# A sliding-window copy kernel: opening load in four DMAs, halved copies placed otherwise, last stores in parts

## Chip, cores, metric

One core of one Trainium2 chip. The metric is the device time of one execution in microseconds (us), smaller is better.

## The reference

```python
# x: (32, 4096, 256) float32, window_size 64, stride 32  ->  out: (32, 127, 64, 256)
for i in range(n_windows):                 # n_windows = (4096 - 64) // 32 + 1 = 127
    start = i * stride
    result[:, i] = x[:, start:start + window_size].copy()
```

There is no arithmetic. A *block* is 32 rows of 256 floats, 32 KB. Window i of a batch is blocks i and i+1, so nearly every block is written twice. 134 MB are read, 266 MB are written.

## The kernel before

The kernel has two ways to move data. Both start and end in HBM, the chip's main memory. Eleven of the 32 batches are *staged*: loaded into SBUF, the core's on-chip memory, once (4 MB, one block a partition) and stored twice, once as first halves and once as second halves of the windows. The other 21 are *direct*: copied from HBM to HBM, 16 windows in one DMA. A staged batch costs the DMA engines three transfers of 4 MB for 8 MB of output, a direct one costs them only the 8 MB of output, but reads every block twice from HBM. (The page of before has 138.41 MB on ScalarE's queue, 33 transfers of 4.19 MB, and 220.95 MB read from HBM: 46.1 by the staged loads, 174.8 by direct copies and edges.) Three queues issue: ScalarE (ACT) the staged loads and stores, SyncE (SP) the direct copies, GpSimd (POOL) at the end the *edges*, windows that a staged store of a neighbouring batch has overwritten with wrong blocks and that must be copied after it.

```python
DIRECT, IN, OUT = 32768, 16384, 16384      # largest piece (descriptor) in bytes

class Staging:
    def load(self, q, g):
        n, i = divmod(g, len(self.tiles))          # 6 tiles
        if n:
            q.wait_ge(self.stored[i], 32 * n)
        self.c.load(q, self.tiles[i], ...).then_inc(self.loaded[i], 16)      # 128 x 32 KB

    def store(self, q, g):
        n, i = divmod(g, len(self.tiles))
        q.wait_ge(self.loaded[i], 16 * (n + 1))
        for half in (0, 1):
            self.c.store(q, self.tiles[i], ..., half, ...).then_inc(self.stored[i], 16)
    # ... run(): six loads, their stores, five loads, their stores
...
    per, loads, stores = 6, 6 * 17, 34
    todo = 7 * len(direct)                          # 147 copies of 16 windows
    turns = share = 0
    with tc.tile_critical():
        st.run(ring_s)                              # ScalarE's queue
        for b in direct:
            w = ...
            for j in range(7):
                todo -= 1
                sem = near if todo == 2 else done
                share += 90 if turns % (loads + per * stores) < loads else 12
                if share >= 120:                    # halved: two DMAs of 16 x 32 KB
                    share -= 120
                    turns += 4
                    count(c.windows(ring_d, b, w, 16, 0), done)
                    count(c.windows(ring_d, b, w, 16, 1), sem)
                else:                               # whole: one DMA of 16 x (2 x 32 KB)
                    turns += 3
                    count(c.windows(ring_d, b, w, 16), sem)
                w += 16
                ...
        ring_r.wait_ge(near, 16)
        ...                                         # edges on GpSimd's queue, each after its stores
        count(c.windows(ring_r, last, 112, 4), rest)
        count(c.columns(ring_r, last, 116, 9), rest)
        st.wait_stored(ring_d, len(staged) - 1)
        count(c.columns(ring_d, last, 125, 2), done)          # 128 KB, after the last store
        for sem in (done, near, rest):
            ring_d.wait_ge(sem, total[sem])
```

`turns` is bookkeeping: a turn is one packet, and a packet that writes a completion counts too. It rests on what the traces show: while both queues are full, they start the same number of packets, 2910 on SyncE's and 2911 on ScalarE's from 150 to 400 us, beside stores, and 1177 and 1173 from 20 to 110 us, beside loads (before, completion writes included). Per engine a whole copy is two data packets and a completion (3 turns for 64 KB), a halved one is 4 turns for 64 KB, a staged load or store is 16 packets of 16 KB and a completion (17 turns for 256 KB). By this counting, halving slows the direct queue against the staged one. The shares fit: beside stores it gives the direct queue 57.8% of the bytes, and 57.6% were measured (before, 150 to 400 us); beside loads, where three of four copies are halved, 53%. With 11 staged batches fixed, halving is the lever by which the kernel sets the mix.

Of the kernel before, what the change touches and what calls it, by code (L numbers as in the profile page):

```python
# [11 lines left out]
class Copier:  # L12


    def __init__(self, x, out, B, L, D, W, S, n_win):
        assert W == 2 * S and L % S == 0
        self.x, self.out = x, out
        self.B = B
        self.blk = S * D
        self.nb = L // S  # L20
        self.nw = n_win
# [24 lines left out]
            in_=self.xap(b * self.nb + w0, [[part, 16], [self.blk, n], row]),  # L46
        )

    def load(self, q, t, b, shift):

        return q.dma_start(
            out=t[:, :],
            in_=self.xap(b * self.nb - shift, [[self.blk, self.nb], [1, self.blk]]),
            max_dma_last_dim=IN,
        )

    def store(self, q, t, b, half, shift):


        w = b * self.nw - half - shift  # L60
        return q.dma_start(
            out=self.oap(2 * w + half, [[2 * self.blk, self.nb], [1, self.blk]]),
            in_=t[:, :],
            max_dma_last_dim=OUT,
        )


class Staging:


    def __init__(self, c, tc, pool, dtype, batches, bufs, shifts):
        self.c, self.batches, self.shifts = c, batches, shifts
        self.tiles = [pool.tile([128, c.blk], dtype, name=f"xb{i}") for i in range(bufs)]
        self.loaded = [tc.alloc_semaphore(f"loaded{i}") for i in range(bufs)]
        self.stored = [tc.alloc_semaphore(f"stored{i}") for i in range(bufs)]

    def shift(self, g):
        return self.shifts.get(self.batches[g], 0)

    def load(self, q, g):  # L80
        n, i = divmod(g, len(self.tiles))
        if n:
            q.wait_ge(self.stored[i], 32 * n)
        self.c.load(q, self.tiles[i], self.batches[g], self.shift(g)).then_inc(self.loaded[i], 16)

    def store(self, q, g):
        n, i = divmod(g, len(self.tiles))
        q.wait_ge(self.loaded[i], 16 * (n + 1))
        for half in (0, 1):
            self.c.store(q, self.tiles[i], self.batches[g], half, self.shift(g)).then_inc(self.stored[i], 16)  # L90

    def wait_stored(self, q, g):
        n, i = divmod(g, len(self.tiles))
        q.wait_ge(self.stored[i], 32 * (n + 1))  # L94

    def run(self, q):
        bufs = len(self.tiles)
        for first in range(0, len(self.batches), bufs):
            group = range(first, min(first + bufs, len(self.batches)))
            for g in group:  # L100
                self.load(q, g)
            for g in group:
                self.store(q, g)


@with_exitstack
def kernel(
    ctx: ExitStack,
    tc: tile.TileContext,
    x: bass.AP,  # L110
    window_size: bass.AP,
    stride: bass.AP,
    out: bass.AP,
):
    nc = tc.nc
    W, S = int(window_size), int(stride)
    B, L, D = x.shape
    n_win = (L - W) // S + 1
    assert out.shape == (B, n_win, W, D)
    c = Copier(x, out, B, L, D, W, S, n_win)  # L120
    staged = [*range(1, B, 3)]
    direct = [b for b in range(B) if b not in staged]
    pool = ctx.enter_context(tc.tile_pool(name="xb", bufs=1))



    st = Staging(c, tc, pool, x.dtype, staged, 6, {0: -1, B - 1: 1})
    ring_d, ring_s, ring_r = nc.sync, nc.scalar, nc.gpsimd
    done = tc.alloc_semaphore("done")
    near = tc.alloc_semaphore("near")  # L130
    rest = tc.alloc_semaphore("rest")
    total = {done: 0, near: 0, rest: 0}

    def count(dma, sem):
        dma.then_inc(sem, 16)
        total[sem] += 16

    per, loads, stores = 6, 6 * 17, 34
    todo = 7 * len(direct)
    turns = share = 0  # L140
    with tc.tile_critical():  # L141
        st.run(ring_s)

        for b in direct:
            w = 0 if b - 1 not in staged else 8 if b + 1 in staged and b + 1 < B - 1 else 15
            for j in range(7):
                todo -= 1
                sem = near if todo == 2 else done
                share += 90 if turns % (loads + per * stores) < loads else 12
                if share >= 120:  # L150
                    share -= 120
                    turns += 4
                    count(c.windows(ring_d, b, w, 16, 0), done)
                    count(c.windows(ring_d, b, w, 16, 1), sem)
                else:
                    turns += 3
                    count(c.windows(ring_d, b, w, 16), sem)
                w += 16
                if todo == 7:
                    count(c.windows(ring_d, B - 1, c.nw - 1, 1, 1, 2048), done)  # L160
                    if 0 in staged:
                        count(c.windows(ring_d, 0, 0, 1, 0, 2048), done)

        ring_r.wait_ge(near, 16)
        pieces = (32768,)
        last = B - 2
        for i, b in enumerate(direct[:-1]):
            for g, n in enumerate(staged):
                if abs(n - b) == 1:
                    st.wait_stored(ring_r, g)  # L170
            parts = [(0, 15)] if b - 1 in staged else [(112, 15)]
            if b - 1 in staged and b + 1 in staged:
                parts = [(0, 8), (120, 7)]
            for w, n in parts:
                count(c.windows(ring_r, b, w, n, None, pieces[i % len(pieces)]), rest)


        count(c.windows(ring_r, last, 112, 4), rest)
        count(c.columns(ring_r, last, 116, 9), rest)
        st.wait_stored(ring_d, len(staged) - 1)  # L180
        count(c.columns(ring_d, last, 125, 2), done)
        for sem in (done, near, rest):
            ring_d.wait_ge(sem, total[sem])


# [33 lines left out]
```

## Time and profile before

Three timed runs: 751.93, 752.80 and 754.36 us.

From the page: the span; the busy share of the 16 DMA engines in 40 equal slices; the rate in GB/s in the same slices; the packets; and each DMA queue with its packets, MB and share of the 16 engines' time (q1 is SyncE's, q10 is ScalarE's, q0 is GpSimd's).

```profile
span 743.6 us, 309 instructions
DMA  9999999999999999999999999999999999999995
GB/s 369 430 429 433 433 437 428 425 422 434 422 420 419 438 423 414 431 428 423 423 431 413 424 427 436 432 426 428 433 425 433 423 427 432 423 426 436 423 428 241
DMA packets 18098, 313.26 MB, mean 421 GB/s; under 512 B 4144, under 2 KB 4144, under 8 KB 4336
q1 hardware_dynamic: 7952, 154.32, 48.9%
q10 hardware_dynamic: 8976, 138.41, 43.9%
q0 software_dynamic: 1168, 20.51, 6.5%
```

The engines are busy for 90% or more of every slice but the last. Only the rate can be improved (slices of 413 to 438), besides the ramp (369) and the end (241). A slice counts a packet's bytes where the packet starts, so single slices scatter; with the bytes spread over each packet's time, the best microsecond is at 433 GB/s.

SyncE's queue: who it waited for, in us in total, how often, the longest. And the last 128 KB copy, from issue to landing:

```profile
SPq L44 <- DMA out_dram<-xb: 179.3, 1, 179.3
out_dram<-in_x_dram SPq DMA_DIRECT2D x1, 128.0 KB, 2.5
```

The queue waits for the last staged store, and only then issues the copy, which lands 2.5 us later on nearly empty engines (24% busy from 735 to 740 us, 2% from there on).

### The profile page before, as it was taken

The page shows a single profiled execution, that of the slowest core. Times are in us where ns is not written, and L with a number is a line of the kernel's source. Part 1 is how long each engine was busy: PE and PEld are TensorE (multiplying, and loading weights), DVE is VectorE, ACT ScalarE, POOL GpSimd, SP SyncE. Part 2 cuts the span into 40 slices and gives each one's busy share as a digit, 9 for nine tenths or more (in the row PEclk, how much of TensorE's full clock was granted, in tenths as well). Part 3 has the DMA queues.
Part 4 walks back from the last instruction along what each step waited for, and adds up shares of the span by engine and source line. Part 5 has one row for each costly group of instructions (what it writes and reads, how often), then busy time and mean ns, then how long its engine had stood idle before and what let it go on. Part 6 is the DMA issues. An engine that isn't in the chain of part 4 may idle for free.

```text
span 743.6 us, 309 instructions
## 1 busy us (share of the span) xinstructions
POOL 12.8 (2%) x26
## 2 busy tenths in 40 slices
POOL 0000000000000000000000000000000000130100
DMA  9999999999999999999999999999999999999995
GB/s 369 430 429 433 433 437 428 425 422 434 422 420 419 438 423 414 431 428 423 423 431 413 424 427 436 432 426 428 433 425 433 423 427 432 423 426 436 423 428 241
DMA packets 18098, 313.26 MB, mean 421 GB/s; under 512 B 4144, under 2 KB 4144, under 8 KB 4336
## 3 DMA queue, kind: packets, MB, share of 16 engines
q1 hardware_dynamic: 7952, 154.32, 48.9%
q10 hardware_dynamic: 8976, 138.41, 43.9%
q0 software_dynamic: 1168, 20.51, 6.5%
q14 instruction: 2, 0.02, 0.0%
HBM read 220.95 MB, written 267.09 MB: 656 GB/s over the span
## 4 chain that ended last, share of the span: by engine, by line
another core or an unknown queue 92%; POOL 2%; issue 0%; POOLq 0%; SPq 0%
POOL out_dram L34 2%; POOL out_dram L44 0%; POOLq L214 0%; SPq L141 0%; POOLq L94 0%
## 5 line engine op out<-in xcount | busy, mean ns | idle before, releaser
L34 POOL DMA_DIRECT2D out_dram<-in_x_dram x21 | 12.0, 576 | 686.7 <-DMA out_dram<-in_x_dram 647.0
L44 POOL DMA_DIRECT2D out_dram<-in_x_dram x1 | 0.6, 581 | 0.0
L200 POOL MEMSET const-float32-0.0<- 128x1 f32 x1 | 0.1, 99 | 0.2 <-issue 0.2
L200 POOL MEMSET const-bfloat16-1.0<- 128x1 bf16 x1 | 0.1, 102 | 0.0
L200 POOL MEMSET const-float32-1.0<- 128x1 f32 x1 | 0.1, 99 | 0.0
L200 POOL MEMSET const-uint8-127<- 128x1 uint8 x1 | 0.1, 99 | 0.0
## 6 DMA issues: line engine op xcount, KB each, us to landing
out_dram<-in_x_dram SPq DMA_DIRECT2D x96, 1024.0 KB, 100.8
out_dram<-xb ACTq DMA_DIRECT2D x22, 4096.0 KB, 142.5
out_dram<-in_x_dram SPq DMA_DIRECT2D x102, 512.0 KB, 89.1
xb<-in_x_dram ACTq DMA_DIRECT2D x11, 4096.0 KB, 122.0
out_dram<-in_x_dram POOLq DMA_DIRECT2D x20, 960.0 KB, 37.8
out_dram<-in_x_dram POOLq DMA_DIRECT2D x1, 576.0 KB, 40.3
out_dram<-in_x_dram POOLq DMA_DIRECT2D x1, 256.0 KB, 36.8
out_dram<-in_x_dram SPq DMA_DIRECT2D x1, 128.0 KB, 2.5
```

The lines of the kernel that those rows point to most:

```text
L34: return q.dma_start(out=self.oap((b * self.nw + w0) * 2 + h, [[2 * blk, n], row]), in_=self.xap(b * self.nb + w0 + h, [[blk, n], row]), m ...
L44: return q.dma_start(out=self.oap((b * self.nw + w0) * 2, [[part, 16], [2 * self.blk, n], row]), in_=self.xap(b * self.nb + w0, [[part, 16 ...
L200: nc = _bacc.Bacc("TRN2", target_bir_lowering=False, num_devices=1)
```

## The change

It is meant to let direct copies begin sooner (the opening load in four DMAs), to place the halved copies anew, above all where loads follow stores, and to take the last 128 KB copy off the end (last stores in parts). The number of staged batches stays 11, and so do all bytes. The core of the diff:

```diff
     def load(self, q, g):
...
+        parts = [(k, 4, 32, 1) for k in range(4)] if g == 0 else [(0, step, n, step)]
+        for rows in parts:                       # (first partition, step, count, ...)
+            self.issue(self.c.load(q, self.tiles[i], b, c, rows), self.loaded[i])
...
     def store(self, q, g):
...
+        parts, end = [((0, step, n, step), 0), ((0, step, n, step), 1)], []
+        if g == len(self.items) - 1:
+            parts = [((0, 1, 128, 1), 1), ((0, 1, 32, 1), 0)]
+            end = [(96, 1, 32, 1)] + [(32 + k, 4, 16, 1) for k in range(4)]
+        for rows, half in parts:
+            self.issue(self.c.store(q, self.tiles[i], b, c, rows, half), self.stored[i])
+        for rows in end:
+            self.issue(self.c.store(q, self.tiles[i], b, c, rows, 0), self.ended)
...
-                share += 90 if turns % (loads + per * stores) < loads else 12
+            second = turns - first_loads - stores
+            loading = turns < first_loads or 0 <= second < loads
+            share += 120 if turns < 16 or -8 <= second < 16 else 90 if loading else 18
...
-        for sem in (done, near, rest):
-            ring_d.wait_ge(sem, total[sem])
+        total[st.ended] = st.count[st.ended]
+        for sem, n in total.items():
+            ring_d.wait_ge(sem, n)
```

Below, *part 1* is the opening load, *part 2* the halves (51 -> 55 of 147 copies), *part 3* the last stores. The rest of the diff rewrites the edges without changing them, and moves one 32 KB copy from near the end of the direct queue to its middle.

More of the change, by code (lines that the diff above doesn't have):

```diff
@@ L47, in columns, with load, store @@
         )
-    def load(self, q, t, b, shift):
+    def load(self, q, t, b, c, rows):
+        p, step, n, unit = rows
         return q.dma_start(
-            out=t[:, :],
-            in_=self.xap(b * self.nb - shift, [[self.blk, self.nb], [1, self.blk]]),
+            out=t[p : p + (n - 1) * step + 1 : step, :],
+            in_=self.xap(b * self.nb + c + p // unit, [[step // unit * self.blk, n], [1, self.blk]]),
             max_dma_last_dim=IN,
         )
-    def store(self, q, t, b, half, shift):
-        w = b * self.nw - half - shift
+    def store(self, q, t, b, c, rows, half):
+        p, step, n, unit = rows
+        w = b * self.nw + c + p // unit - half
         return q.dma_start(
-            out=self.oap(2 * w + half, [[2 * self.blk, self.nb], [1, self.blk]]),
-            in_=t[:, :],
+            out=self.oap(2 * w + half, [[2 * step // unit * self.blk, n], [1, self.blk]]),
+            in_=t[p : p + (n - 1) * step + 1 : step, :],
             max_dma_last_dim=OUT,
@@ L68, with __init__ @@
 class Staging:
-    def __init__(self, c, tc, pool, dtype, batches, bufs, shifts):
-        self.c, self.batches, self.shifts = c, batches, shifts
+    def __init__(self, c, tc, pool, dtype, items, bufs):
+        self.c, self.items = c, items
         self.tiles = [pool.tile([128, c.blk], dtype, name=f"xb{i}") for i in range(bufs)]
@@ L75, in __init__ @@
         self.stored = [tc.alloc_semaphore(f"stored{i}") for i in range(bufs)]
-    def shift(self, g):
-        return self.shifts.get(self.batches[g], 0)
-    def load(self, q, g):
-        n, i = divmod(g, len(self.tiles))
-        if n:
-            q.wait_ge(self.stored[i], 32 * n)
-        self.c.load(q, self.tiles[i], self.batches[g], self.shift(g)).then_inc(self.loaded[i], 16)
-    def store(self, q, g):
-        n, i = divmod(g, len(self.tiles))
-        q.wait_ge(self.loaded[i], 16 * (n + 1))
-        for half in (0, 1):
-            self.c.store(q, self.tiles[i], self.batches[g], half, self.shift(g)).then_inc(self.stored[i], 16)
+        self.ended = tc.alloc_semaphore("ended")
@@ new lines, in __init__, with issue @@
+        self.count = {sem: 0 for sem in (*self.loaded, *self.stored, self.ended)}
+        self.after_load, self.after_store = {}, {}
+    def issue(self, dma, sem):
+        dma.then_inc(sem, 16)
+        self.count[sem] += 16
+    def load(self, q, g):
+        i = g % len(self.tiles)
+        b, c, n = self.items[g]
+        if self.count[self.stored[i]]:
+            q.wait_ge(self.stored[i], self.count[self.stored[i]])
+        step = 128 // n
+        parts = [(k, 4, 32, 1) for k in range(4)] if g == 0 else [(0, step, n, step)]
+        for rows in parts:
+            self.issue(self.c.load(q, self.tiles[i], b, c, rows), self.loaded[i])
+        self.after_load[g] = self.count[self.loaded[i]]
@@ new lines, in store @@
+    def store(self, q, g):
+        i = g % len(self.tiles)
+        b, c, n = self.items[g]
+        q.wait_ge(self.loaded[i], self.after_load[g])
+        step = 128 // n
+        parts, end = [((0, step, n, step), 0), ((0, step, n, step), 1)], []
[6 more added lines that the diff above has]
+            self.issue(self.c.store(q, self.tiles[i], b, c, rows, 0), self.ended)
+        self.after_store[g] = self.count[self.stored[i]]
@@ L92, in wait_stored @@
     def wait_stored(self, q, g):
-        n, i = divmod(g, len(self.tiles))
-        q.wait_ge(self.stored[i], 32 * (n + 1))
+        q.wait_ge(self.stored[g % len(self.tiles)], self.after_store[g])
     def run(self, q):
         bufs = len(self.tiles)
-        for first in range(0, len(self.batches), bufs):
-            group = range(first, min(first + bufs, len(self.batches)))
+        for first in range(0, len(self.items), bufs):
+            group = range(first, min(first + bufs, len(self.items)))
@@ L121 @@
     staged = [*range(1, B, 3)]
+    items = [(b, -1 if b == B - 1 else 0, c.nb) for b in staged]
+    place = {b: g for g, (b, _, n) in enumerate(items) if n == c.nb}
     direct = [b for b in range(B) if b not in staged]
     pool = ctx.enter_context(tc.tile_pool(name="xb", bufs=1))
-    st = Staging(c, tc, pool, x.dtype, staged, 6, {0: -1, B - 1: 1})
+    st = Staging(c, tc, pool, x.dtype, items, 6)
     ring_d, ring_s, ring_r = nc.sync, nc.scalar, nc.gpsimd
@@ L136, in count @@
         total[sem] += 16
-    per, loads, stores = 6, 6 * 17, 34
-    todo = 7 * len(direct)
+    sixteens = []
+    for b in direct:
+        w = 15 if b - 1 in staged else 0
+        sixteens += [(b, w + 16 * j) for j in range((c.nw - w) // 16)]
+    singles = [(B - 1, c.nw - 1, 1)]
+    edges = [(b, 0 if b - 1 in staged else 112, 15) for b in direct[:-1]]
+    last = B - 2
+    edges.append((last, 112, 4))
+    first_loads, loads, stores = 6 * 17, 5 * 17, 6 * 34
     turns = share = 0
@@ L142 @@
         st.run(ring_s)
-        for b in direct:
-            w = 0 if b - 1 not in staged else 8 if b + 1 in staged and b + 1 < B - 1 else 15
-            for j in range(7):
-                todo -= 1
-                sem = near if todo == 2 else done
-                share += 90 if turns % (loads + per * stores) < loads else 12
-                if share >= 120:
-                    share -= 120
-                    turns += 4
-                    count(c.windows(ring_d, b, w, 16, 0), done)
-                    count(c.windows(ring_d, b, w, 16, 1), sem)
-                else:
-                    turns += 3
-                    count(c.windows(ring_d, b, w, 16), sem)
-                w += 16
-                if todo == 7:
-                    count(c.windows(ring_d, B - 1, c.nw - 1, 1, 1, 2048), done)
-                    if 0 in staged:
-                        count(c.windows(ring_d, 0, 0, 1, 0, 2048), done)
@@ L164 @@
-        ring_r.wait_ge(near, 16)
-        pieces = (32768,)
-        last = B - 2
-        for i, b in enumerate(direct[:-1]):
-            for g, n in enumerate(staged):
-                if abs(n - b) == 1:
-                    st.wait_stored(ring_r, g)
-            parts = [(0, 15)] if b - 1 in staged else [(112, 15)]
-            if b - 1 in staged and b + 1 in staged:
-                parts = [(0, 8), (120, 7)]
-            for w, n in parts:
-                count(c.windows(ring_r, b, w, n, None, pieces[i % len(pieces)]), rest)
@@ L178 @@
-        count(c.windows(ring_r, last, 112, 4), rest)
+        for i, (b, w) in enumerate(sixteens):
+            sem = near if i == len(sixteens) - 2 else done
+            second = turns - first_loads - stores
+            loading = turns < first_loads or 0 <= second < loads
+            share += 120 if turns < 16 or -8 <= second < 16 else 90 if loading else 18
+            if share >= 120:
+                share -= 120
+                turns += 4
+                count(c.windows(ring_d, b, w, 16, 0), done)
+                count(c.windows(ring_d, b, w, 16, 1), sem)
+            else:
+                turns += 3
+                count(c.windows(ring_d, b, w, 16), sem)
+            if i == len(sixteens) // 2:
+                for b, w, half in singles:
+                    count(c.windows(ring_d, b, w, 1, half, 2048), done)
@@ L179 @@
+        ring_r.wait_ge(near, 16)
+        for b, w, n in edges:
+            for k in (b - 1, b + 1):
+                if k in place and b != last:
+                    st.wait_stored(ring_r, place[k])
+            count(c.windows(ring_r, b, w, n), rest)
         count(c.columns(ring_r, last, 116, 9), rest)
-        st.wait_stored(ring_d, len(staged) - 1)
+        st.wait_stored(ring_d, place[B - 1])
         count(c.columns(ring_d, last, 125, 2), done)
-        for sem in (done, near, rest):
-            ring_d.wait_ge(sem, total[sem])
+        total[st.ended] = st.count[st.ended]
```

## The prediction

> What bounds it. The engine table shows only POOL, 2% busy. The slices show the 16 DMA engines 9 tenths busy or more in 39 of 40, 313.26 MB at a mean of 421 GB/s. The packet records give 430 to 432 GB/s while staged loads run beside direct copies, about 425 (400 to 432) beside staged stores. [...] its best microseconds are at 433. At 432, 313.26 MB need 725 us; data packets run for 739. The other 14 us (estimates from packet records):
> - Start: 79, 221, 400, 425 GB/s in the first four microseconds of packets, about 1.4 us lost; the first 16 KB packets take 1.2 to 1.6 us, later ones 0.61.
> - Store stretches: 32 KB direct packets take 1.24 us instead of 1.21; about 7 us.
> - End: 427 down to 10 GB/s over the last six microseconds, about 4.5 us. The slowest of the 16 engines is 3 to 4 us behind, and falls behind beside stores, not loads (one DMA's 16 landings spread by 0.5 to 0.8 us in the first loads, over 3 us by the second). After the last store lands (SyncE queue's wait, 179 us), a 128 KB copy is issued and takes 2.5 us, alone.
>
> What the change does. Bytes are the same: 147 direct copies of 16 windows, 11 batches, the same edges (the changed edge rule never applied to this spacing). Three things move.
> 1. Opening load in four DMAs. Before, the first direct packet starts 3.8 us after the first load packet, though issued 0.05 us after it[...]. In quarters it should come about 1 us after. But loads alone already ran at 400 GB/s from the third microsecond, so only the ramp can be filled: 0 to 0.6 us.
> 2. Halved copies 51 -> 55: all halved where the second loads start, 15% instead of 10% beside stores. [...] one packet, completion writes included, is a turn: beside loads that predicts 47:53, measured 204 to 226 GB/s. Beside stores the direct share moves only from 57.8 to 57.4%. Both queues already empty within about 2 us of each other: -0.3 to +0.3 us[...].
> 3. Last stores in parts. What the final copy overwrites is stored first and counted; 96 rows (3.1 MB, about 17 us at that queue's 185 GB/s) follow on another semaphore. The 128 KB copy runs under them. This is on the critical path: the end was 751.1 on the trace's clock, while the edge copies had landed at 749.8; its bytes cost 0.3 us in the stream. Gain 0.9 us. The lagging engine has the same bytes and still ends last.
>
> Sum: 0.3 + 0 + 0.9, and some tuning of the mix that I can't cost: about 1.8 us of 752.8, 0.24%.
>
> Predicted 751.0 us, 748.6 to 752.7 in 8 of 10. Faster by over 2%: 1%; within 2%: 98%; slower: 1%.
>
> What would show it: 313.3 MB again; first direct packet 1 to 2 us after the first load packet; SyncE's queue not waiting for the last store at the very end, its 128 KB copy landing over 10 us before it; last slice up from 241 towards 265 GB/s; middle slices 413 to 438.
>
> What would make it wrong: the extra halves leave one queue alone at the end for several us; store stretches gain or lose some us[...]; the small parts at the end land late on the lagging engine.

Where the text is marked as cut, a claim stood that no trace of this case shows: a ceiling for the rate, an order in which queues are served, what the first direct packet waits for, and an effect of addresses. 0.3 + 0 + 0.9 us, and 0.6 us for the tuning, make the 1.8 us. That a packet is a turn rests on the equal counts above. "About 1 us after" in step 1 was the author's estimate.

## The result

Ratios here and below are the mean time of one kernel's fast runs over that of the other's of the same rounds, with a 95% interval; they are not quite the ratios of the medians.

| | before | changed | ratio |
|---|---|---|---|
| first job | 752.03 us (6 runs, 751.92 to 754.36) | 751.36 us (6 runs, 750.73 to 754.35) | 0.9991 (0.9971 to 1.0012) |
| repeated, 5 rounds | 752.48 us (11 runs) | 752.84 us (5 runs) | 1.0002 (0.9990 to 1.0014) |

The changed kernel is neither faster nor slower. The page of the changed kernel, the same lines:

```profile
span 749.4 us, 322 instructions
DMA  8999999999999999999999999999999999999996
GB/s 360 401 427 429 427 429 428 434 423 418 420 424 423 418 424 415 422 427 427 414 427 417 429 432 429 430 422 430 429 423 421 423 421 419 425 426 423 431 409 262
DMA packets 18290, 313.26 MB, mean 418 GB/s; under 512 B 4336, under 2 KB 4336, under 8 KB 4528
q1 hardware_dynamic: 8016, 154.32, 48.8%
q10 hardware_dynamic: 9104, 138.41, 44.0%
q0 software_dynamic: 1168, 20.51, 6.5%
```

```profile
SPq L44 <- DMA out_dram<-xb: 170.3, 1, 170.3
out_dram<-in_x_dram SPq DMA_DIRECT2D x1, 128.0 KB, 9.4
```

Bytes are equal, packets are 192 more, which are completion writes: 12 more DMAs on 16 engines. The opening slices are slower (360 and 401 against 369 and 430), the slice before the last is slower (409 against 428), the last is faster. The copy of 128 KB now takes 9.4 us to land, but under the stores.

Taken alone, these two pages say that the change costs 5.8 us; the clock says that it costs nothing. The repeats below settle which to believe.

### The profile page after: what moved, and what is told of

It reads as the page before. It is cut to its first block, busy times and chain, and to the rows that moved or that the text cites. A ratio compares the mean times of both kernels' runs of the same rounds, so it can differ in the third digit from the quotient of the medians.

```text
span 749.4 us, 322 instructions
## 1 busy us (share of the span) xinstructions
POOL 12.8 (2%) x26
## 2 busy tenths in 40 slices
DMA packets 18290, 313.26 MB, mean 418 GB/s; under 512 B 4336, under 2 KB 4336, under 8 KB 4528
## 3 DMA queue, kind: packets, MB, share of 16 engines
HBM read 220.95 MB, written 267.09 MB: 651 GB/s over the span
## 4 chain that ended last, share of the span: by engine, by line
another core or an unknown queue 92%; POOL 2%; issue 0%; POOLq 0%; SPq 0%
POOL out_dram L34 2%; POOL out_dram L44 0%; POOLq L236 0%; SPq L172 0%; POOLq L114 0%
```

## The experiments

Twelve kernels were run, all correct. The runs c_before to t4_after shared one job, p1_only to p3_ports a second, ports_half to p23 a third, p3_two a fourth.

### c_before, c_after: the two kernels again

No edit.

> The kernel before against itself. Every theory: ratio 1.000 within the noise of the rounds (about 0.2%). It shows the noise, and how far one profile can be trusted: the profiled span of before was 743.6 us, that of after 749.4 us, although the timed runs differ by less than 1 us the other way. If profiles repeat (theory: the change costs 5.8 us that the profile sees), this profile's span is 743.6 within 1 us and its 16 KB packets beside loads (20 to 130 us of the span) again take 0.61 us on average; if the span is a matter of the run (rival), it lies anywhere from 743 to 752.

> The changed kernel again, with more rounds. Prediction's theory: 0.5 to 2 us faster than before (ratio 0.997 to 0.9995). If the longer profile of after was a property of the kernel, the profiled span is again about 749 and the load stretch again loses about 2 us; if of the run, it lies elsewhere.

Measured: before against itself 1.0000 (0.9987 to 1.0013), which is the noise; the changed kernel 1.0002. The spans and rates of the two pages, before first:

```profile
span 751.2 us, 309 instructions
GB/s 370 428 425 421 431 424 418 425 420 426 421 419 419 418 425 416 422 414 427 421 414 417 414 428 431 432 416 424 430 425 425 421 419 433 418 427 423 428 420 246
```

```profile
span 751.2 us, 322 instructions
GB/s 356 422 431 428 421 418 427 429 425 419 421 425 425 416 428 418 421 431 421 420 421 408 429 435 425 423 431 429 425 419 420 428 415 421 421 427 422 427 409 245
```

The same kernel has a span of 743.6 us on one page and of 751.2 us on another. So the rival was right: the 5.8 us between the first two pages were of the executions, not of the kernels. (In the third job the kernel before ran at 744.85 to 745.82 us in nine runs, with spans of 743.1 to 744.0, which is where the first page's 743.6 lies; in the other jobs it ran at medians of 750.9 to 752.8. Each job had another chip; whether it is the chip, or where the arrays lie, no run shows.) From here on traces of one job are set against each other where there are any; comparisons across jobs are named as such and are weaker.

From the packet records one can keep a ledger: at a given time since the span's start, how far the bytes moved are behind a steady 432 GB/s, in us. Two traces of before (c_before and t4_before, which is the same kernel up to its last microseconds) and two of the changed kernel (c_after, t4_after), all of one job:

| us lost against 432 GB/s | before | changed | difference of the means |
|---|---|---|---|
| 0 to 40 us | 3.12, 3.21 | 4.03, 4.11 | +0.9 |
| 40 to 130 | 2.10, 1.38 | 1.59, 1.70 | -0.1 |
| 130 to 430 (stores) | 8.38, 8.21 | 6.88, 6.80 | -1.5 |
| 430 to 545 (second loads) | 1.23, 0.81 | 1.18, 1.11 | +0.1 |
| 545 to 720 (stores, edges) | 3.56, 3.62 | 4.16, 4.37 | +0.7 |
| 720 to the last data (c_ runs only) | 4.45 | 4.66 | +0.2 |

So the change does move time on this chip: about 1.5 us are won in the long store stretch, and lost again in the opening and towards the end. The same shows in the windows of the profile (from, to, length, GpSimd's busy time, clock, DMA share, GB/s; a share can pass 1.00, as a packet's whole time counts where it starts), before first:

```profile
0.00:6.00 6.00, 0.20 (x4) 1.00 0.72 262
20.00:40.00 20.00, 0.00 (x0) 1.00 0.99 422
130.00:430.00 300.00, 0.00 (x0) 1.00 1.01 420
545.00:720.00 175.00, 12.55 (x22) 1.00 1.01 424
720.00:735.00 15.00, 0.00 (x0) 1.00 1.00 425
```

```profile
0.00:6.00 6.00, 0.20 (x4) 1.00 0.67 246
20.00:40.00 20.00, 0.00 (x0) 1.00 0.99 418
130.00:430.00 300.00, 0.00 (x0) 1.00 1.01 422
545.00:720.00 175.00, 12.55 (x22) 1.00 1.01 422
720.00:735.00 15.00, 0.00 (x0) 1.00 1.01 404
```

The last line is the telling one: 425 GB/s before, 404 after, in the stretch where the stores of part 3 are cut small.

### t4_before, t4_after: the last copy four times

```diff
-        count(c.columns(ring_d, last, 125, 2), done)
+        for again in range(4):
+            if again:
+                ring_d.wait_ge(done, total[done])
+            count(c.columns(ring_d, last, 125, 2), done)
```

> Before, with its last 128 KB copy made four times, each waiting for the one before: the suspected cost of part 3 (a copy alone at the end) three times over. Theory (that copy is on the critical path at about 2.5 us a piece): 3 x 2.5 = 7.5 us longer, ratio 1.010. Rival (its latency overlaps with the end of the program or the lagging engine): under 2 us longer.

> The changed kernel with the same copy made four times, each waiting for the one before. Theory (17 us of stores still run behind it, so it is off the critical path): at most 1 us longer than the changed kernel, from three times 128 KB at 430 GB/s = 0.9 us. Rival (under load each copy takes 4 to 8 us to land, so that four in a row outlast the stores): 5 us or more longer.

Measured: 759.13 us, ratio 1.0094 (1.0079 to 1.0110), so 7.1 us for three more copies in the kernel before, 2.4 us each; the trace has 2.41 to 2.48 us from each issue to the next. The copy at the end is on the critical path, as the theory had it. In the changed kernel: 756.21 us, 1.0051 (1.0031 to 1.0070), which is 3.7 us over the changed kernel's own 1.0002, where the theory allowed 1. Its first copy, under full engines, took 9.8 us from issue to the next issue, the second 5.4, the last two 2.5 each: four in a row outlast the stores, as the rival had it. SyncE's waits between the four copies (us in total, how often, the longest), t4_before, then t4_after:

```profile
SPq L44 <- DMA out_dram<-in_x_dram: 5.6, 3, 1.9
```

```profile
SPq L44 <- DMA out_dram<-in_x_dram: 16.0, 3, 9.2
```

The one copy that the changed kernel really makes does not: it was issued 731.5 us into the span and landed 9.2 us later, 6.9 us ahead of the last data. Part 3 does what it was made for.

### p1_only, p2_only, p3_only: each part alone, on the kernel before

```diff
# p1_only
-        self.c.load(q, ..., self.shift(g)).then_inc(self.loaded[i], 16)
+        for rows in [(k, 4, 32) for k in range(4)] if g == 0 else [(0, 1, 128)]:
+            self.c.load(q, ..., self.shift(g), rows).then_inc(self.loaded[i], 16)
# p2_only
-                share += 90 if turns % (loads + per * stores) < loads else 12
+                second = turns - 306
+                loading = turns < 102 or 0 <= second < 85
+                share += 120 if turns < 16 or -8 <= second < 16 else 90 if loading else 18
# p3_only
-        for half in (0, 1):
-            ...then_inc(self.stored[i], 16)
+        parts = [(0, (0, 1, 128), self.stored[i]), (1, (0, 1, 128), self.stored[i])]
+        if g == len(self.batches) - 1:
+            parts = [(1, (0, 1, 128), self.stored[i]), (0, (0, 1, 32), self.stored[i])]
+            parts += [(0, r, self.ended) for r in [(96, 1, 32)] + [(32 + k, 4, 16) for k in range(4)]]
+        for half, rows, sem in parts:
+            self.c.store(q, ..., half, ..., rows).then_inc(sem, 16)
```

> Before with part 1 alone (opening load in four DMAs of every fourth partition). In the two traces of the changed kernel the first load packet came 4.0 us after the span's start instead of 2.0, the first direct packet at 2.4 instead of 5.8, and by 40 us the bytes moved are 4.0 to 4.8 us behind a steady 432 GB/s instead of 3.1. Theory A (part 1 costs about what part 3 gains): 0.5 to 1.5 us slower, ratio 1.0007 to 1.002, and the trace is 4.0 or more behind at 40 us. Prediction (part 1 gains 0 to 0.6 us): ratio 0.999 to 1.000, under 3 behind at 40 us.

> Before with part 2 alone (the new places of the halved copies). Prediction: -0.3 to +0.3 us, ratio 0.9995 to 1.0005. Rival (halves beside stores ease the store stretches): the stretch from 130 to 430 us loses 1 us less than the 8.2 to 8.4 us of the repeats of before, ratio 0.998 to 0.999.

> Before with part 3 alone (last stores in parts). Prediction: 0.9 us faster, ratio 0.9988. Theory B (the two parts of 32 neighbouring partitions [...]slow all packets of some 12 us by 5 to 15%): the gain is given back, ratio 0.9995 to 1.0005, and in the trace 16 KB and 32 KB packets 15 to 10 us before the end take over 0.64 and 1.3 us as in the changed kernel (0.61 and 1.22 in before).

| | median us | ratio to before | lost 0 to 40 us | lost 130 to 430 us |
|---|---|---|---|---|
| before (11 runs, same job) | 750.85 | | | |
| p1_only | 752.42 | 1.0014 (0.9998 to 1.0030) | 4.49 | 8.03 |
| p2_only | 750.37 | 0.9991 (0.9978 to 1.0004) | 3.27 | 6.41 |
| p3_only | 750.38 | 0.9995 (0.9983 to 1.0008) | 3.39 | 6.95 |

No single interval is clear of 1, so the clock alone decides nothing here. With the ledger:

**Part 1 costs about 1 us.** All four traces with the load in four parts are 4.0 to 4.8 us behind at 40 us; all traces with it in one are 3.1 to 3.4 behind. Theory A is what the ledger shows. Two causes are visible. In p1_only the first packet starts later, 2.42 us into the span instead of 2.00 (the first of the four issues takes 0.70 us, the one issue 0.41), and at 6 us p1_only is 0.4 us further behind than before. And packets are slower while the four parts run: 32 KB direct packets that start between 5 and 28 us take 1.225 to 1.240 us on average in the four traces with it, 1.215 to 1.216 in six traces without it (before, c_before, t4_before, p2_only, p3_only, p3_ports). What slows them is not shown. One candidate is the mix, the subject of theory C below: in those 23 us the direct queue has 59.8% of the bytes in p1_only and 56.4 to 56.5% in the changed kernel, against 53.1 to 53.3% in the three traces of before.

It doesn't even start the direct copies sooner by itself. The queues in the first 6 us of c_before, then c_after, then p1_only (packets that start, MB, share of the engines' time):

```profile
q10 hardware_dynamic: 80, 1.31, 62.0%
q1 hardware_dynamic: 8, 0.26, 10.2%
```

```profile
q10 hardware_dynamic: 48, 0.79, 35.3%
q1 hardware_dynamic: 37, 0.69, 31.3%
```

```profile
q10 hardware_dynamic: 64, 1.05, 52.3%
q1 hardware_dynamic: 16, 0.52, 21.0%
```

In p1_only the first direct packet comes at 5.5 us, as in before (5.7 to 5.8); in p2_only, whose first copies are halved, at 5.7. Only in the changed kernel, with both, does it come at 2.4 us, and then ahead of the first load packet, which slips to 4.05. There the bytes gained by one queue are lost by the other, and the sum is smaller: 1.47 MB against 1.57 (c_before).

**Part 2 seems to gain in the store stretch.** From 130 to 430 us 6.4 to 6.9 us are lost in all four traces with the new halves of the slower jobs, 7.0 to 8.9 in the six with the old ones. That is the rival's side of its expectation, in p2_only 1.9 us under the repeats of before. But the other old-halves traces of its own job are only 0.5 to 1.6 us worse, and differ by 1.1 us among themselves, though they have the same instructions in this stretch; one trace of p2_only doesn't settle it. The mechanism that fits is the mix: the direct queue's share of the bytes from 150 to 400 us is 57.7% in c_before (60.79 of 105.27 MB) and 57.4% in c_after (60.72 of 105.73).

**Part 3 alone** gains 0.4 us as the best estimate, with an interval that holds both 0 and the predicted 0.9. Its end is slow as theory B said: ScalarE's 16 KB packets take 0.653 us and GpSimd's 32 KB packets 1.293 us on average from 20 to 10 us before the last staged or edge packet (0.614 and 1.229 in c_before).

### p3_ports, ports_half, ports_all: do neighbouring partitions cost?

Theory B laid the slow end on the parts of 32 neighbouring partitions. The reason that the expectations gave for it is shown by no trace of this case and is cut from them; what is left, and was tested, is that such parts are slow. In the expectation of ports_all the two cases are that parts spread over the partitions cost nothing, and that they still cost something.

```diff
# p3_ports: against p3_only
-            parts = [(1, (0, 1, 128), self.stored[i]), (0, (0, 1, 32), self.stored[i])]
-            parts += [(0, r, self.ended) for r in [(96, 1, 32)] + [(32 + k, 4, 16) for k in range(4)]]
+            parts = [(1, (0, 1, 128), self.stored[i]), (0, (0, 4, 32), self.stored[i])]
+            parts += [(0, r, self.ended) for r in [(k, 4, 32) for k in range(1, 4)]]
# ports_half: against before, every staged store        ports_all: rows (k, 4, 32) instead
-            self.c.store(q, ..., half, ...).then_inc(self.stored[i], 16)
+            for k in range(4):
+                self.c.store(q, ..., half, ..., (32 * k, 1, 32)).then_inc(self.stored[i], 16)
```

> Part 3 alone with parts of every fourth partition (0, 4, ... 124, then 1, 5, ... and so on, four parts of 32 rows) in place of neighbouring ones. Theory B: packets 15 to 10 us before the end back at 0.61 to 0.62 and 1.21 to 1.25 us, and about 0.8 us faster than part 3 alone, ratio to before 0.9985 to 0.9992. Rival (any small parts slow the end, or it is luck): packets as slow as in part 3 alone, no faster.

> Before with every staged store cut into four DMAs of 32 neighbouring partitions (0 to 31, 32 to 63 and so on): 22 stores of 4 MB instead of the 2 MB of part 3. Theory B[...]: the slowing of part 3's two such parts (about 0.9 us for 2 MB) grows to 15 to 45 us, ratio 1.02 to 1.06, and the stores' 16 KB packets take 0.65 us or more on average from 140 to 410 us (0.617 in before). Rival (the slow microseconds near the end had another cause[...]): only the cost of 66 more completion writes an engine and a changed mix, under 4 us, packets at 0.61 to 0.63.

> The same number of DMAs, each of every fourth partition (k, k+4, ... k+124), as the opening load of the change has them. [...]: within 4 us of before and packets at 0.61 to 0.63. [...] (what the slower packets of the opening load in parts suggest, direct copies 1.22 to 1.24 us against 1.215 in the first 28 us): packets at 0.63 to 0.66 and 5 to 30 us slower, but less than ports_half.

Measured: p3_ports 750.96 us, 0.9998 (0.9985 to 1.0012), packets 0.643 and 1.269 us near the end: a little better than p3_only there, not as in before, and no faster. ports_half 774.45 us, 1.0391 (1.0368 to 1.0414); ports_all 756.52 us, 1.0152 (1.0138 to 1.0166); before in that job 745.09 us.

The totals look like a win for theory B, and they aren't. The queues from 150 to 400 us, where direct copies run beside the stores, of ports_half, then ports_all:

```profile
DMA packets 6075, 104.08 MB, mean 416 GB/s; under 512 B 1681, under 2 KB 1681, under 8 KB 1681
q1 hardware_dynamic: 3038, 64.16, 62.1%
q10 hardware_dynamic: 3037, 39.91, 38.5%
```

```profile
DMA packets 6059, 103.90 MB, mean 416 GB/s; under 512 B 1673, under 2 KB 1673, under 8 KB 1673
q1 hardware_dynamic: 3031, 64.07, 62.1%
q10 hardware_dynamic: 3028, 39.83, 38.4%
```

They are the same but for a tenth of a per cent, and so is the mean 16 KB packet from 140 to 420 us (0.629 and 0.630 us). Expected for theory B was 0.65 or more in one of them alone. Beside direct copies, neighbouring partitions cost nothing that shows. A difference shows where the staged queue runs nearly alone (85 and 93% of the engines' time), as the direct one has finished early. Twenty microseconds near the end, ports_half (708 to 728 us), then ports_all (709 to 729):

```profile
DMA packets 520, 7.05 MB, mean 352 GB/s; under 512 B 125, under 2 KB 125, under 8 KB 125
q10 hardware_dynamic: 451, 5.90, 84.9%
```

```profile
DMA packets 645, 8.83 MB, mean 442 GB/s; under 512 B 133, under 2 KB 133, under 8 KB 133
q10 hardware_dynamic: 601, 7.95, 93.2%
```

There neighbouring partitions go with the lower rate, 352 against 442 GB/s, which is the direction of theory B. It is not proof of it: the two kernels also write rows 64 KB and 256 KB apart in HBM, and no run separates that. Part 3's small stores have edge copies beside them (2.65 MB of edges with 1.41 MB of stores in 10 us of p3_only), and with spread partitions (p3_ports) the stretch from 20 to 10 us before the end is slow as well, so theory B does not explain that stretch. The last microseconds stay open: from 720 us to the last data p3_ports loses 2.6 us and p3_only 4.3, and the slowest of the 16 engines ends its last store 1.6 us after the median one against 3.2. That is one trace each, and the clock shows no gain.

What both kernels share is the other half of the finding. Four DMAs instead of one give the staged queue four completion writes instead of one, 20 turns instead of 17 for the same bytes. The direct queue's share of the bytes from 150 to 400 us went from 57.6% (the first trace of before, a run as fast as this job's) to 61.6 and 61.7%, and the rate fell from 425 to 416 GB/s. Counting turns gives the same: 20 for 256 KB staged beside 3.1 on average for 64 KB direct make 61.7%, 17 make 57.8%. The own time of the completion writes is not what costs: one takes 9 ns in the records, together 0.96 us per engine in these 250 us against 0.68 in before, while the lower rate costs over 5 us. That led to theory C.

### p23: the changed kernel without part 1

```diff
-        parts = [(k, 4, 32, 1) for k in range(4)] if g == 0 else [(0, step, n, step)]
+        parts = [(0, step, n, step)]
```

> The changed kernel with the opening load in one DMA again: parts 2 and 3 without part 1. If the parts add up (measured alone: part 1 +1.4, part 2 -0.9, part 3 -0.5 parts in a thousand), 1.0 us faster than before, ratio 0.998 to 0.9995, and about 1.1 us faster than the changed kernel's 1.0002. The trace is 3.0 to 3.5 us behind 432 GB/s at 40 us. Rival (the parts' figures are noise): ratio 1.000.

Measured: 747.42 us against 745.09, ratio 1.0024 (1.0010 to 1.0037). It is slower, where the sum of the parts said 1.0 us faster; the expectation failed with its rival. The ledger of its opening is as expected (3.08 at 40 us). Set against the first trace of before, from another job but equally fast, p23 loses 0.7 us more from 545 to 720 us and 1.5 us more from there to the last data. With 20 us to go before the last staged or edge packet the staged queue has 1.29 MB left and GpSimd's queue 4.75 MB; in the first trace of before 3.15 and 4.11. The likely reason: part 1, by letting direct copies in first, had set the staged queue back (3.1 MB moved by 20 us instead of 4.2), and parts 2 and 3 are set for that. Without it the staged queue is done early, the edge copies have 71% of the bytes from 20 to 10 us before the end, and the rate is 384 GB/s. So the parts do not add up. That they are tuned against each other fits, but is not proven: it is one trace, the changed kernel did not run in this job, and the slowest engine here ends its last store 6.3 us after the median one (3.5 in c_after), which may be a loss of its own.

### p3_two: part 3 with fewer parts

Theory C: what a small store costs is a turn, whatever partitions it reads. Each part's completion write takes a turn of the staged queue, the direct or edge queue gets more of the bytes, and stretches with a larger direct share run slower (425 GB/s at 57.6% in before, 416 at 61.7% in ports_all). If so, the second half of the last batch in two DMAs in place of six should end the slow stretch.

```diff
# against p3_only
-            parts = [(1, (0, 1, 128), self.stored[i]), (0, (0, 1, 32), self.stored[i])]
-            parts += [(0, r, self.ended) for r in [(96, 1, 32)] + [(32 + k, 4, 16) for k in range(4)]]
+            parts = [(1, (0, 1, 128), self.stored[i]), (0, (0, 1, 16), self.stored[i])]
+            parts += [(0, r, self.ended) for r in [(16, 1, 112)]]
```

> Before with the last batch's second stored half in two DMAs (16 rows, counted for the final copy, then 112 rows) instead of six. Theory C (what the small parts cost is turns: each part adds a completion write that takes a turn of its queue, so from 20 to 10 us before the end the direct copies' share of the bytes rose from 54-55% to 62-64%, and stretches with a larger direct share run slower, 425 GB/s at 57.6% and 416 at 61.7%): direct share 54 to 59% there, packets at 0.61 to 0.63 and 1.21 to 1.26 us, rate 420 GB/s or more, and the whole gain of part 3: 0.9 us, ratio 0.998 to 0.9995. Rival (storing the second half first, or the copy under the stores, is itself what slows the end): share as in before but packets at 0.65 and 1.3 us as in part 3 alone, ratio 0.9995 to 1.0005. If theory C holds this version beats both kernels.

From 20 to 10 us before the last staged or edge packet, from the packet records:

| | direct and edge share of bytes | GB/s | 16 KB stores, us | 32 KB edges, us | rate x (1 + share): GB/s through HBM |
|---|---|---|---|---|---|
| c_before | 53.8% | 428 | 0.614 | 1.229 | 658 |
| p3_two | 57.4% | 425 | 0.622 | 1.240 | 669 |
| p3_ports | 62.4% | 412 | 0.643 | 1.269 | 668 |
| p3_only | 63.4% | 404 | 0.653 | 1.293 | 661 |
| c_after | 64.8% | 392 | 0.666 | 1.342 | 646 |
| p23 | 71.4% | 384 | 0.693 | 1.376 | 658 |

The rows come from all four jobs, one trace each. The queues in those 10 us of c_before, c_after, p3_two and p23 (these views count a packet where it starts, the table splits it at the edges of the 10 us, so the rates differ by up to 3%):

```profile
q0 software_dynamic: 118, 2.29, 54.1%
q10 hardware_dynamic: 123, 2.02, 47.2%
```

```profile
q0 software_dynamic: 119, 2.39, 61.5%
q10 hardware_dynamic: 122, 1.41, 36.1%
q1 hardware_dynamic: 23, 0.09, 2.5%
```

```profile
q0 software_dynamic: 118, 2.46, 58.4%
q10 hardware_dynamic: 108, 1.74, 41.2%
q1 hardware_dynamic: 32, 0.12, 3.0%
```

```profile
q0 software_dynamic: 127, 2.72, 71.6%
q10 hardware_dynamic: 102, 1.10, 29.2%
```

c_before and c_after start about as many packets on q10 (123 and 122), but in c_after many are completion writes, and they carry 1.41 MB instead of 2.02. Theory C is borne out for the stretch: share, packet times and rate of p3_two are within what it said, and storing the second half first, which p3_two does too, is not to blame.

The last column: a staged byte crosses HBM once in a transfer, a direct or edge byte twice (313.26 MB in all and 174.83 of them direct or edge make 488.1; the page of before has 220.95 MB read and 267.09 written, 488.0). The sum stays within 646 to 669 GB/s while the rate goes from 384 to 428; in the store stretch it is 664 (c_before) and 665 (c_after), in ports_all 672. That speaks for HBM as the limit once the direct share is over some 54% (an estimate: 664 GB/s through HBM at 432 GB/s of DMA traffic); it is an inference from these sums, no experiment changed HBM traffic alone. No run here got above 673 from 150 to 400 us.

The time, however: 753.78 us against 752.83, ratio 1.0004 (0.9986 to 1.0021). The gain of 0.9 us did not show, nor is it excluded. In this trace the slowest engine ended its last store 4.6 us after the median one (3.6 in c_before), and the last data came 4.9 us later than 432 GB/s would have it from 720 us on (4.5 in c_before). This is the part that stays open: the slowest engine's lag behind the median one at its last store ran from 1.6 us (p3_ports) to 6.3 us (p23), one trace each, and no run separates its causes. No version beat the kernel before clearly.

## Why the prediction was right, and where it wasn't

The time was right: 751.0 predicted with 748.6 to 752.7, 751.36 measured, "within 2%" with 98%. Bytes, middle slices and the waits came as predicted. The size of the gain was not: -1.8 us predicted, -0.7 (interval -2.2 to +0.9) in the first job and +0.2 (-0.8 to +1.1) in the repeat, worked out as (ratio - 1) x 752. The hit is in part luck: the stated range also holds 752.03 us, the time of the kernel before in the same job, and steps that were wrong in opposite directions cancelled. Step by step:

- **"so only the ramp can be filled: 0 to 0.6 us" (part 1).** The reason was right, loads alone do fill the engines (0.98 busy from 2 to 5 us in before). The sign was wrong: +0.9 us by the ledger of one job. Cutting the load has costs that the step left out: a later first packet (2.42 us into the span in p1_only instead of 2.00) and slower packets for the 25 us that the parts take (direct ones 1.225 to 1.240 us instead of 1.215 to 1.216). "First direct packet 1 to 2 us after the first load packet" was wrong too: the direct packet came 1.6 us before the load packet, with parts 1 and 2 together, and as late as before with part 1 alone. Nor does the whole first load, 256 packets, have to go first: 80 load packets had started when the first direct one came in before, and 64 in p1_only, where the first part is no longer than that.
- **"-0.3 to +0.3 us" (part 2).** The predicted shares, 57.8 to 57.4%, were measured as 57.7 to 57.4%. What such a step is worth was mis-sized: the prediction valued it by when the two queues empty, not by the rate, and the stretch from 130 to 430 us loses 1.5 us less. From 150 to 400 us, where the shares were read, it is 1.0 us less. If the sum through HBM is what is limited, at 664 GB/s, 664 / 1.577 = 421.1 and 664 / 1.574 = 421.9 GB/s differ by 0.2%, which is 0.5 us of 250: the direction, and about half of the size. Another 0.4 us lie between 400 and 430 us, where the copies halved before the second loads take the direct share from 56 to 51.5%. About 0.7 us were given back from 545 to 720 us, and the mix does not explain that: the direct share rose from 57.1 to 57.7% between 570 and 640 us, but fell from 57.1 to 56.1% over the whole stretch. That loss stays open.
- **"Gain 0.9 us" (part 3).** The copy is off the end: in c_before it ended 1.2 us after the edges had landed, in c_after the end is that of the edges. What was left out is the price of the five additional DMAs in the last stores, each with its completion writes: 10 us at 392 instead of 428 GB/s are 0.8 us. That fewer of them end the slow stretch is what p3_two shows, in one trace. That "the lagging engine [...] still ends last" held.
- **"its 128 KB copy landing over 10 us before it"**: 6.9 us before the last data (10.5 us before the end of the span), since it took 9.2 us to land under load. **"last slice up from 241 towards 265 GB/s"**: 262 on the first page; but in the repeat 245 against 246.
- **"some tuning of the mix that I can't cost"** was counted as a gain of 0.6 us. p23 suggests that the tuning holds the parts together; no run shows a gain on top.

Of the stated dangers, "the extra halves leave one queue alone" resembles what p23 ran into once part 1 was gone. The net zero is thus, by the ledger of one job, a sum of terms near 1 us, +0.9, -1.5, +0.7 and smaller ones. The loss in the opening showed in all four traces with part 1. The gain in the store stretch showed in two traces against two of one job; the first pair of pages, 5.8 us apart in span, has it the other way round (5.0 us lost before, 6.6 after). The terms of the end did not repeat as well.

## What to carry to other kernels

When two queues keep the DMA engines full, ask what cutting a transfer into smaller ones does to the mix: here 20 packets instead of 17 for 256 KB of stores, the additional ones completion writes, moved the direct queue's share of the bytes from 57.6 to 61.7%, the rate from 425 to 416 GB/s and the time by +1.5% (ports_all, the shares and rates against the first trace of before). Before taking a serial piece off the end, ask what the cuts that allow it do to the stretch before it; and test parts of a tuned mix together, because their effects need not add up. Never set one profile against one profile for differences below a per cent: here the same kernel had spans of 743.6 and 751.2 us, and only a ledger of several traces of one job began to tell the effects apart.
